# Loading b21 behind the third piece of a22, and b11's units in the order of their loading

## The chip, the core and the metric

The kernel runs on one core of one Trainium2 chip. The core has five engines with a queue of instructions each: TensorE (PE in the profile; matrix products), VectorE (DVE), ScalarE (ACT), GpSimd (POOL) and SyncE (SP). They run side by side and wait for each other by semaphores; within one engine the order of the program holds. Transfers between device memory and the on-chip memory are issued from the queues of SP, ACT and POOL, and 16 DMA engines carry them out. The metric is the time of one execution on the device in microseconds.

## The reference

```python
def reference(a, b, alpha):          # a, b: 4096 x 4096 float32, alpha = 0.01
    x = np.matmul(a, b)
    return np.where(x > 0, x, alpha * x)
```

A product of two square matrices, and a leaky ReLU on it.

## The kernel before

The output is cut into regions of 1024 x 1024. `g` (0 to 3) counts 1024 rows of A, called a group here, `j` (0 to 3) 1024 columns of B. The first region, (0, 0), is computed plainly. The other fifteen are taken in the order of the list `regions`: (0,1), (0,2), (0,3), then for each later group the columns 2, 0, 3, 1, and in the last group 2, 0, 1, 3. Counted from 0, regions 3, 7 and 11 are the first of their groups, 4, 8 and 12 the second, and 2, 6 and 10 are the "turning" ones, in which the next group of A comes in. The flags `turning`, `first_of_group` and `second_of_group` say so in the code.

A region is computed by Winograd's form of Strassen's method, with seven products instead of eight. A's part is cut into a11, a12, a21, a22 (512 rows by 2048 of k) and B's into b11, b12, b21, b22 (2048 of k by 512 columns). Sums of the quarters of A are s1 to s4, and sums of the quarters of B are made in place by DVE (`b_sum`, line 589), so that the tile of b11, for instance, holds b11 for product 0, then the sum t2 for product 2, then the sum for product 4. The products are listed in order:

```python
PRODUCTS = [("a11", 0, 0), ("a12", 1, 0), ("s2", 0, 0), ("s3", 0, 1), ("s1", 0, 0), ("a22", 1, 0), ("s4", 1, 1)]
```

Each entry names the operand of A and the quarter of B (half of k, half of the columns). Product 1 is a12 by b21, product 5 a22 by the sum that stands in b21's place. In regions that are not turning, and past group 0, some products are split once more into quarters of 256 (`fourth_in_quarters`, `sixth_in_quarters`, `seventh_in_quarters`, with the matmuls on line 752). Whole products have their matmuls on line 807: 64 of 128x128 by 128x512.

Every quarter of B has two units, k = 0 and 1, of 1024 rows of k: a tile of 128 x 8 x 512 in float16, 1 MB, in `b_pool`. A tag (`b11`, `b12`, `b21`, `b22`) has two buffers, so the two units of the next region's quarter take the buffers of the two units of this region's, and each load waits for the last product that reads its buffer. The variable `ks` is the order in which a region walks the units: (0, 1), or (1, 0) where the region before it was in quarters. So regions 4, 8 and 12 walk 1, 0; so do regions 6 and 10, while 7 and 11 walk 0, 1.

The order of the work is written by hand: every engine's queue has the order in which the code is written. `fetch_b(i + 1, quads, ks)` loads quarters of the next region's B through `fetch_unit`. For column 2 (`CACHED`), which is the first column of each later group, a unit comes from a float16 copy that an earlier region has left in device memory, as one transfer of 1 MB on SP's queue (line 528). For other columns it comes from B itself on POOL's queue, with the cast to float16 (line 533), or from another kept copy.

The next group of A comes in while a turning region is computed. It comes in four quarters of four pieces, 128 rows by 2048 of k each, in float16 0.5 MB. `fetch_a` issues a piece as four transfers on POOL's queue (line 133), into one of three buffers `a16`. `turn_a_in` transposes it on DVE (two instructions of line 142) and squares it on ACT (line 608; sums of squares that are tested later). `bring_a(1, 1, range(3))` does this for the first three pieces of a22, which is the last quarter to come in; the fourth follows after it.

What stands around the change is the end of a turning region. In the order of the code: product 4; the leaky ReLU and stores of one quarter of the output; `fetch_b` of b11; product 5 and its addition to the output quarter u2; `fetch_b` of b21; the three pieces of a22; `leave(u2_pairs, 1, 0)`, which runs the leaky ReLU on u2 (two DVE instructions, line 313) and issues four stores on SP (line 984); the sums of squares, the fourth piece and the sums s1 and s2 of the next group; product 6; `fetch_b` of b22; the copies of product 6's four PSUM banks on ACT (`keep`, line 820); and the last stores. The next region's product 1 writes the banks that these copies empty.

The order on SP at a turn is thus: b11 (two loads), b21 (two loads), the four stores of u2, b22 (two loads), four stores.

A small write by DVE has been used before to hold a load back: `load_s2(g, k, later=True)` sets one column of the tile on DVE (line 770), and the load that follows waits for it, and so for all that stands before it in DVE's queue. That load is on SP too.

Product 0 of regions past the first of a group is ordered by unit, then by pairs of row tiles:

```python
if n == 0 and late_s2:
    order = [(mt, k, c) for k in ks for mts in ((0, 1), (2, 3)) for c in range(KC) for mt in mts]
```

In regions 4, 8 and 12, b11 was loaded by the first region of the group, which walks its units 0, 1; product 0 walks them 1, 0. After product 0, DVE's sums go over the units in the order `ks` (lines 1049 to 1055): b12 minus b22 for a unit, then that added into b11 for the same unit.

Of the kernel before, what the change touches and what calls it, by code (L numbers as in the profile page):

```python
# [24 lines left out]
KC = 8  # L25
# [23 lines left out]
def kernel(  # L49
# [17 lines left out]
    nc = tc.nc  # L67
# [108 lines left out]
    def rows_of(mat, u, c, wide, whole):  # L176

        if u >= 2 or whole:
            per = 2 * KC
            k0 = u // 2 * 2 * KW  # L180
            c += u % 2 * KC
        else:
            per = KC // RUNS[u]
            k0 = u * KW + c // per * per * P
        return mat[k0:k0 + per * P, :].rearrange("(p c) n -> p c n", p=P)[:, c % per:c % per + wide, :]

    def b_rows(j, u, c, wide, nt=None, whole=False):

        n0 = j * 2 * NT + (nt or 0) * NT
        return rows_of(b[:, n0:n0 + (2 * NT if nt is None else NT)], u, c, wide, whole)  # L190
# [4 lines left out]
    def place(g, h, mt, j, nt):  # L195
        row = ((g * 2 + h) * MT + mt) * P
        col = (j * 2 + nt) * NT
        return out[row:row + P, col:col + NT]
# [4 lines left out]
    def a_cols(t, c, mt, is_plain=False):  # L203
        rows = slice(mt * P, (mt + 1) * P)
        return plain(t)[:, c, rows] if is_plain else t[:, c // 2, rows, c % 2]
# [106 lines left out]
    def leaky(t):  # L312
        nc.vector.scalar_tensor_tensor(t, t, alpha, t, op0=MULT, op1=MAX if alpha <= 1 else MIN)  # L313
# [24 lines left out]
    order = [("b", 0), ("a", 0, 0, 1), ("a", 1, 0, 1), ("a", 2, 0, 1), ("a", 3, 0, 1)]  # L338
# [3 lines left out]
    for what, i, *more in order:  # L342
        if what == "a":
            r, tiles = more
            k = slice(r * rw, (r + 1) * rw)
# [106 lines left out]
    for i in range(1, len(steps)):  # L452
        t, h, u, first, last = steps[i]
# [19 lines left out]
        t, h, u, first, last = steps[i]  # L473
# [34 lines left out]
    def fetch_b(i, quads, ks):  # L508

        if i >= len(regions):  # L510
            return
        for half, nt in quads:
            for k in ks:
                fetch_unit(i, 2 * half + k, nt)

    def move_t(name, t, k, out, queue=nc.sync):
        ends = kept_t[name][k], t.rearrange("p c n -> p (c n)")
        queue.dma_start(*(ends if out else ends[::-1]))

    def fetch_unit(i, u, nt):  # L520
        g, j = regions[i]
        half = u // 2
        t = b_pool.tile([P, KC, NT], DT, name="b", tag=f"b{half + 1}{nt + 1}")
        have_b[i, u, nt] = t
        if g > 1 and j == CACHED and (half, nt) == (0, 1):
            move_t("t3", t, u, False)
        elif g and j == CACHED:
            nc.sync.dma_start(t, rows_of(kept[nt], u, 0, KC, True))
        elif half and (g and j == LAST or g > 1 and j in OTHERS):
            nc.sync.dma_start(t.rearrange("p c n -> p (c n)"), kept_half[j][u - 2, nt])  # L530
        else:
            for c in range(0, KC, 4):
                nc.gpsimd.dma_start(t[:, c:c + 4, :], b_rows(j, u, c, 4, nt, g > 0))  # L533
            if j == CACHED:
                wide = KC // (RUNS + [1, 1])[u]
                for c in range(0, KC, wide):
                    nc.sync.dma_start(rows_of(kept[nt], u, c, wide, False), t[:, c:c + wide, :])
# [44 lines left out]
    def operand(g, name, k):  # L582
        if name[0] == "s":
            return s[g, name, k]
        return at[g, int(name[1]) - 1, 2 * (int(name[2]) - 1) + k]
# [5 lines left out]
    def measure(i, which, x, y):  # L591

        if which:
            tiles = [have_b[i, 2 * x + k, y] for k in ((1, 0) if regions[i][0] else (0, 1))]
        else:
            tiles = [at[regions[i][0], x, 2 * y + k] for k in range(2)]
        parts = halves(tiles[0]) + halves(tiles[1])
        if tiles[0] is first_a:
            return MeasureFirst(which, parts, None)
        return Measure(which, parts, not which)  # L600
# [181 lines left out]
    in_quarters = False  # L782
    for i, (g, j) in enumerate(regions):

        ks = (1, 0) if in_quarters else (0, 1)
        late_s2 = in_quarters
        final = i == len(regions) - 1
        turning = i + 1 < len(regions) and regions[i + 1][0] != g
# [8 lines left out]

        def product(n, banks, first):
            name, half, nt = PRODUCTS[n]
            todo = [(k, c) for k in ks for c in range(KC)]  # L800
            order = [(mt, k, c) for k, c in todo for mt in range(MT)]
            if n == 0 and late_s2:

                order = [(mt, k, c) for k in ks for mts in ((0, 1), (2, 3)) for c in range(KC) for mt in mts]
            for mt, k, c in order:
                t = operand(g, name, k)
                nc.tensor.matmul(  # L807
                    banks[mt], a_cols(t, c, mt, t is first_a), B(half, nt, k)[:, c, :],
                    start=first and (k, c) == todo[0], stop=(k, c) == todo[-1], skip_group_check=not first,
                )  # L810
# [160 lines left out]
        def add(acc, banks):  # L971
            for to, bank in zip(acc, banks):
                nc.vector.tensor_add(to, bank, to)  # L973
# [6 lines left out]
        def leave(pairs, h, nt):  # L980
            for r, t in enumerate(pairs):
                leaky(t.rearrange("p m n -> p (m n)"))
                for m in range(2):
                    nc.sync.dma_start(place(g, h, 2 * r + m, j, nt), t[:, m, :])

        if i == 0:
            for u, nt in ((2, 0), (2, 1), (3, 0), (3, 1)):
                fetch_unit(0, u, nt)
            for to, kept_part in stores:
                nc.gpsimd.dma_start(to, kept_part)  # L990
            sum_a(g, "s1")
            sum_a(g, "s2")
# [20 lines left out]
        def bring_a(h, half, some=range(MT)):  # L1013
            if turning:
                for n in some:
                    fetch_a(h, half, n)
                    turn_a_in(h, half, n)
# [7 lines left out]
        in_quarters = g > 0 and not turning  # L1025
        in_fourth = in_quarters and not first_of_group
        second_of_group = in_fourth and regions[i - 2][0] != g
# [3 lines left out]
        if first_of_group and g:  # L1031
            keep_s2(g)

        product(0, y, True)
        if second_of_group:
            sums_of_s3(g, (2,))
# [5 lines left out]
        if have_t2:  # L1042
            for k in ks:
                t = have_b[i, k, 0] = b_pool.tile([P, KC, NT], DT, name="b", tag="b11")
# [23 lines left out]
        bring_a(0, 0, range(3 if g else 4))  # L1068

        product(1, z, True)  # L1070
        add(u1, z)
        leave(u1_pairs, 0, 0)
# [25 lines left out]
        if not g:  # L1098
            bring_a(0, 1)

        product(2, y, False)
        if late_ones:
            late_ones[0].begin()
        u2_pairs, u2 = keep(y, 1 - side)
        if g:
            t = x_pool.tile([P, 4, QUARTER], DT, name="q", tag="x")
# [79 lines left out]
        if not in_quarters:  # L1186
            product(5, z, g > 0)
            add(u2[::-1], z[::-1])
        fetch_b(i + 1, [(1, 0)], (1, 0) if in_quarters else ks)
        bring_a(1, 1, range(3))  # L1190
        leave(u2_pairs, 1, 0)
        if sixth:
            sixth = measure(i + sixth[0], *sixth)
            sixth.begin()
            sixth.end()
# [33 lines left out]
    with tc.If(even == 0):  # L1229
        for m in range(M // RM):  # L1230
            a_blocks = []
            for u in range(KU):
                t = a_pool.tile([P, KC // 2, RM, 2], BF16, name="a", tag=f"a{u // 2 + 1}{m % 2 + 1}")
# [6 lines left out]
            for n in range(N // NT):  # L1240
                banks = [new_bank(n % 2 * 4 + mt) for mt in range(MT)]
                cols = slice(n * NT, (n + 1) * NT)
                for u in range(KU):
                    t = b_pool.tile([P, KC, NT], BF16, name="b", tag=f"b{u // 2 + 1}{n % 2 + 1}")
# [8 lines left out]
                for mt in range(MT):  # L1253
                    t = c_pool.tile([P, 2, NT], FP32, name="c", tag=f"c{side}")[:, 0]
# [44 lines left out]
```

## Time and profile before

| | us |
|---|---|
| median of 3 runs | 1534.99 (1533.63 to 1537.55) |
| the profiled execution's own time | 1536.2 |
| its span in the profile | 1534.2 |
| TensorE busy | 1524.3 |
| DVE busy | 1158.9 |
| ACT busy | 425.5 |
| POOL busy | 258.5 |

All times in the profile are counted from the start of the span. TensorE's granted clock is 0.999 of full speed. The matmuls are pipelined, and the end of one is modelled, so waits on TensorE are better read from the distance between starts. The regions that the change touches start on TensorE at these times: region 2 at 314.4, 3 at 411.1, 4 at 505.2, 6 at 689.5, 7 at 784.6, 8 at 878.1, 10 at 1062.1, 11 at 1157.6, 12 at 1251.7. The b loads that a line of the profile calls `b<-kept` are those from the kept copy; `a<-in_a_dram` are quarters of pieces of A. In the bytes by queue, `q1` is SP's queue, `q0` POOL's, `q10` ACT's.

### The profile page before, as it was taken

What the parts mean: (1) busy time and instruction counts of PE and PEld (TensorE: products, weight loads), DVE (VectorE), ACT (ScalarE), POOL (GpSimd) and SP (SyncE); (2) the same over time, 40 slices, a digit from 0 to 9 for tenths busy, and PEclk for the clock granted to TensorE, in tenths of its full rate; (3) what the DMA queues carried; (4) which work ended last, traced back from release to release, by engine and by line L of the source; (5) the groups of instructions that cost most, each with busy time, mean ns of one, the idle gap of its engine ahead of it and who ended that gap; (6) DMA issues with size and microseconds to landing.
All of it is one profiled execution on the core that took longest, in us unless ns stands there. A gap on an engine that the chain in (4) does not pass through costs nothing. (4 is left out here: it accounts for less than half of the span.)

```text
span 1534.2 us, 21785 instructions
## 1 busy us (share of the span) xinstructions
PE 1524.3 (99%) x8667; PEld 847.1 (55%) x8667; DVE 1158.9 (76%) x1207; ACT 425.5 (28%) x730; POOL 258.5 (17%) x426
## 2 busy tenths in 40 slices
PE   9999999999999999999999999999999999999998
PEld 4444444444446567574544747557544475746656
DVE  4368867765699686768769698676976987687677
ACT  2201344646310213103641130312464103041210
POOL 5641110143202011022220001010331100101000
PEclk9999999999999999999999999999999999999999
DMA  9999995998879999899797939669899892948723
GB/s 246 186 215 203 237 281 169 180 197 172 231 277 287 258 278 275 251 289 255 170 288 266 321 148 208 260 157 322 166 241 283 235 349 72 294 162 190 301 97 140
DMA packets 192002, 351.26 MB, mean 229 GB/s; under 512 B 18705, under 2 KB 131601, under 8 KB 178834
## 3 DMA queue, kind: packets, MB, share of 16 engines
q0 software_dynamic: 119808, 112.22, 46.2%
q1 hardware_dynamic: 65458, 211.98, 37.0%
q10 hardware_dynamic: 6624, 25.56, 4.4%
q8 instruction: 70, 1.15, 0.3%
q14 instruction: 42, 0.34, 0.1%
HBM read 344.98 MB, written 114.82 MB: 300 GB/s over the span
## 5 line engine op out<-in xcount | busy, mean ns | idle before, releaser
L807 PE MATMUL ps<-b,a 128*128 128x512 f16 x2624 | 571.1, 379 | 0.5 <-DMA b<-in_b_dram 0.3
L807 PE MATMUL ps<-b,s 128*128 128x512 f16 x2240 | 489.2, 379 | 0.0
L807 PEld LDWEIGHTS <-a 128*128 128x128 f16 x2624 | 256.7, 98 | 308.8 <-issue 1.5
L807 PEld LDWEIGHTS <-s 128*128 128x128 f16 x2240 | 219.1, 98 | 262.5 <-issue 0.4
L589 DVE TENSOR_TENSOR b<-b 128x4096 f16<-128x4096 f16 x104 | 234.6, 2286 | 42.7 <-DMA b<-in_b_dram 34.1
L533 POOL DMA_DIRECT2D b<-in_b_dram x128 | 94.9, 746 | 860.1 <-PE ps L752 437.2
L820 ACT COPY c<-ps 128x512 f32<-128x512 f32 x164 | 84.8, 596 | 469.1 <-PE ps L807 433.3
L142 DVE STREAM_TRANSPOSE a<-a 128x512 uint32<-128x512 uint32 (+2 forms) x120 | 127.0, 1106 | 100.8 <-DMA a<-in_a_dram 100.8
L133 POOL DMA_DIRECT2D a<-in_a_dram x252 | 137.6, 554 | 266.8 <-ACT junk L608 98.2
L608 ACT ACTIVATE junk<-a 128x512 bf16<-128x512 f16 x192 | 121.1, 631 | 99.1 <-DMA a<-in_a_dram 93.8
L752 PEld LDWEIGHTS <-q 128*128 128x128 f16 x1424 | 139.3, 98 | 16.7 <-issue 0.6
L313 DVE SCALAR_TENSOR_TENSOR c<-c 128x1024 f32<-128x1024 f32 (+2 forms) x123 | 141.5, 1190 | 3.8 <-ACT c L820 3.5
L973 DVE TENSOR_TENSOR c<-ps,c 128x512 f32<-128x512 f32 x140 | 87.5, 682 | 55.5 <-PE ps L807 41.8
L231 ACT ACTIVATE sq<-b 128x2048 bf16<-128x2048 f16 x64 | 118.3, 1910 | 37.1 <-DVE sq L240 29.4
L752 PEld LDWEIGHTS <-a 128*128 128x128 f16 x1200 | 117.4, 98 | 18.0 <-issue 0.4
L283 PE MATMUL ps<-b,a 128*128 128x512 f16 x512 | 112.4, 379 | 0.6 <-DVE part L324 0.2
L752 PE MATMUL ps<-b,q 128*128 128x256 f16 x784 | 92.0, 273 | 0.4 <-DVE c L862 0.4
L752 PE MATMUL ps<-b,a 128*128 128x256 f16 x752 | 88.3, 273 | 0.0
L283 PEld LDWEIGHTS <-a 128*128 128x128 f16 x512 | 49.7, 98 | 61.2 <-issue 2.1
L909 ACT COPY c<-ps 128x512 f32<-128x512 f32 x9 | 5.3, 586 | 269.7 <-PE ps L752 148.3
L752 PEld LDWEIGHTS <-s 128*128 128x128 f16 x624 | 61.0, 98 | 7.1
L862 DVE TENSOR_TENSOR c<-ps,c 128x512 f32<-128x512 f32 x80 | 52.2, 683 | 14.4 <-PE ps L752 14.4
(104 smaller groups left out, 904.8 us busy)
## 6 DMA issues: line engine op xcount, KB each, us to landing
b<-in_b_dram POOLq DMA_DIRECT2D x136, 512.0 KB, 11.7
out_dram<-c SPq DMA_DIRECT2D x240, 256.0 KB, 6.3
a<-in_a_dram POOLq DMA_DIRECT2D x244, 128.0 KB, 5.8
b<-kept_half SPq DMA_DIRECT2D x28, 1024.0 KB, 10.9
b<-kept SPq DMA_DIRECT2D x20, 1024.0 KB, 9.2
q<-kept_qs ACTq DMA_DIRECT2D x40, 512.0 KB, 7.8
s<-kept_s SPq DMA_DIRECT2D x18, 1024.0 KB, 7.7
q<-kept_qa SPq DMA_DIRECT2D x28, 512.0 KB, 7.3
```

The source lines that it names most:

```text
L133: nc.gpsimd.dma_start(a16[32 * q:32 * q + 32], src.rearrange("(g i) w -> i g w", i=32))
L142: nc.vector.transpose(part.rearrange("p c m e -> p c (m e)").bitcast(U32) .rearrange("p c (g i) -> p g c i", i=32), src[:, :, i * n:(i + 1 ...
L231: nc.scalar.activation(to, self.parts[n], SQUARE)
L283: nc.tensor.matmul(ps, a_cols(at[0, h, u], c, mt, (h, u) == (0, 0)), bt[0, u, nt][:, c, :], start=first, stop=last,)
L313: nc.vector.scalar_tensor_tensor(t, t, alpha, t, op0=MULT, op1=MAX if alpha <= 1 else MIN)
L533: nc.gpsimd.dma_start(t[:, c:c + 4, :], b_rows(j, u, c, 4, nt, g > 0))
L589: nc.vector.tensor_tensor(f(to), f(x0), f(x1), op)
L608: nc.scalar.activation(junk, piece[:, q, :], SQUARE, accum_out=to[:, 4 * n + q:4 * n + q + 1])
L752: nc.tensor.matmul(to[m], xq[:, c // 2, rows, c % 2], yq[:, c, :], start=first and c == 0 and m < banks, stop=c == KC - 1, skip_group_chec ...
L807: nc.tensor.matmul(banks[mt], a_cols(t, c, mt, t is first_a), B(half, nt, k)[:, c, :], start=first and (k, c) == todo[0], stop=(k, c) == t ...
L820: nc.scalar.copy(kept[mt], banks[mt])
L973: nc.vector.tensor_add(to, bank, to)
```

## The change

In turning regions the two loads of the next region's b21 are no longer issued right after product 5, but after the three pieces of a22 and the leaky ReLU and stores of u2. Each is preceded by a write of one column of its tile on DVE, so that SP issues the load only when DVE has come to that point. Other regions keep their order.

In product 0 of the second region of a group the units are walked 0, 1 instead of 1, 0. The DVE sums after it keep their order.

```diff
-    def fetch_unit(i, u, nt):
+    def fetch_unit(i, u, nt, later=False):
         g, j = regions[i]
         half = u // 2
         t = b_pool.tile([P, KC, NT], DT, name="b", tag=f"b{half + 1}{nt + 1}")
         have_b[i, u, nt] = t
+        if later:
+            nc.vector.memset(t[:, :1, :1], 0.0)
...
         def product(n, banks, first):
             name, half, nt = PRODUCTS[n]
-            todo = [(k, c) for k in ks for c in range(KC)]
+            ks_here = (0, 1) if n == 0 and second_of_group else ks
+            todo = [(k, c) for k in ks_here for c in range(KC)]
             order = [(mt, k, c) for k, c in todo for mt in range(MT)]
             if n == 0 and late_s2:
-                order = [(mt, k, c) for k in ks for mts in ((0, 1), (2, 3)) for c in range(KC) for mt in mts]
+                order = [(mt, k, c) for k in ks_here for mts in ((0, 1), (2, 3)) for c in range(KC) for mt in mts]
...
-        fetch_b(i + 1, [(1, 0)], (1, 0) if in_quarters else ks)
+        if not turning:
+            fetch_b(i + 1, [(1, 0)], (1, 0) if in_quarters else ks)
         bring_a(1, 1, range(3))
         leave(u2_pairs, 1, 0)
+        if turning:
+            for k in ks:
+                fetch_unit(i + 1, 2 + k, 0, True)
```

## The prediction

> **What bounds the kernel now.** I read the page's busy table first, then TensorE's timeline for gaps, then, around the three places where a group of A comes in, the timelines of DVE, SP and POOL, and the bytes by queue.
>
> ```profile
> span 1534.2 us, 21785 instructions
> PE 1524.3 (99%) x8667; PEld 847.1 (55%) x8667; DVE 1158.9 (76%) x1207; ACT 425.5 (28%) x730; POOL 258.5 (17%) x426
> ```
>
> The next lines are TensorE's timeline: start, length, line, tiles, count, and in brackets an idle time.
>
> ```profile
> 507.38 26.06 PE L807 MATMUL ps<-b,a 128*128 128x512 f16 x120 [0.31 <-DMA b<-in_b_dram]
> ...
> 784.62 27.79 PE L807 MATMUL ps<-b,a 128*128 128x512 f16 x128
> ...
> 1157.55 28.38 PE L807 MATMUL ps<-b,a 128*128 128x512 f16 x128
> ```
>
> TensorE is the bound, and it hardly ever waits. 128 matmuls of 512 columns take 27.79 us (0.216 us each) in region 7 and 28.38 us in region 11: 0.6 us of waiting, where product 1 of region 11 needs the PSUM banks that ScalarE copies out at 1170.5 to 1172.6. The bracket at 507.38 is region 4 waiting for the last piece of b11; by the starts of the matmuls on both sides the hole is 0.47 us. From 107 us to the end I find seven holes by start-to-start times, 2.1 us together. Nothing that only takes waits away can gain more than these 2.1 us, 0.14%.
>
> Now the third turn (regions 10 to 11), with the lines of SP, DVE and POOL in that order, each in a fence of its own:
>
> ```profile
> 1138.36 2.58 SPq L984 DMA_DIRECT2D out_dram<-c  x4
> 1141.17 3.08 SPq L528 DMA_DIRECT2D b<-kept  x4
> 1169.83 1.97 SPq L984 DMA_DIRECT2D out_dram<-c  x4
> 1171.89 1.00 SPq L528 DMA_DIRECT2D b<-kept  x2
> ```
>
> ```profile
> 1161.62 2.12 DVE L142 STREAM_TRANSPOSE a<-a 128x512 uint32<-128x512 uint32 x2 [13.54 <-DMA a<-in_a_dram]
> 1164.03 2.11 DVE L142 STREAM_TRANSPOSE a<-a 128x512 uint32<-128x512 uint32 x2 [0.29 <-DMA a<-in_a_dram]
> 1166.59 2.11 DVE L142 STREAM_TRANSPOSE a<-a 128x512 uint32<-128x512 uint32 x2 [0.45 <-DMA a<-in_a_dram]
> 1168.61 2.33 DVE L313 SCALAR_TENSOR_TENSOR c<-c 128x1024 f32<-128x1024 f32 x2
> ```
>
> ```profile
> 1142.04 4.29 POOL L133 DMA_DIRECT2D a<-in_a_dram  x8 [3.91 <-ACT junk L608]
> 1151.93 0.54 POOL L133 DMA_DIRECT2D a<-in_a_dram  x1 [5.61 <-DMA a<-in_a_dram]
> 1154.92 0.55 POOL L133 DMA_DIRECT2D a<-in_a_dram  x1 [2.45 <-DMA a<-in_a_dram]
> 1158.81 0.54 POOL L133 DMA_DIRECT2D a<-in_a_dram  x1 [3.35 <-DMA a<-in_a_dram]
> 1161.78 0.55 POOL L133 DMA_DIRECT2D a<-in_a_dram  x1 [2.43 <-DMA a<-in_a_dram]
> ```
>
> The x4 of SP at 1141.17 are b11 (two units) and b21 (two units); the x2 at 1171.89 are b22. DVE sits idle 13.5 us until the first piece of a22 is there. POOL has issued eight quarter pieces and the next four go out one at a time, each when an earlier one has landed: eight are in flight at most. The bytes by queue say why the pieces are slow; first the stretch 1146 to 1152, with b on SP's queue (q1) beside a on POOL's (q0), then 1158 to 1161, a alone:
>
> ```profile
> q1 hardware_dynamic: 262, 1.88, 78.3%
> q0 software_dynamic: 249, 0.24, 25.1%
> ...
> q0 software_dynamic: 623, 0.57, 115.9%
> ```
>
> Beside b, A gets 0.04 MB/us; alone 0.19. A piece is 0.5 MB.
>
> **The change, part by part.** Working against the profiled execution: its own time is 1536.2 us, 2.0 above its span and 1.2 above the median of 1534.99.
>
> *b21 moved behind the a22 pieces (three turns).* Removed from their place: six SP issues of 1 MB. Added: six memsets on DVE, 59 ns each by the nine rows of line 770, 0.12 us a turn. They run right after the leaky of u2; DVE has 13.5 us of idle time shortly before, so they cost TensorE nothing, and without that cover 0.35 us. POOL's and ScalarE's queues keep their orders. On SP the four u2 stores no longer stand behind b21 (no gain, they wait for the leaky); b22's two loads and the next stores now stand behind b21.
>
> First, how much earlier is a22? Up to the landing of b11's second unit nothing changes, since b21 is behind b11 on the same queue. By the landing records that unit is in at 777.4 (second turn) and 1150.6 (third) on the median DMA engine; on the last, 778.2 and 1152.2. Of twelve quarter pieces one is in by then and the second a quarter or less. The rest come at 0.128 MB / 0.19 = 0.65 us each (the landings in that stretch are 0.6 to 0.65 apart): some 10.8 x 0.65 = 7.0 us, so the median engine ends at 784.4 and 1157.6. The slowest engine lags 1.1 in the second turn and 1.7 in the third at that point. POOL's pacing is no limit: the twelfth issue needs the fourth quarter landed, 780.3 and 1154.1, and 2.6 us to the first bytes. So the third piece is in at 785.5 and 1159.3; before it was 790.6 and 1166.5. In the first turn, in the same way, 408.3 instead of 413.5.
>
> Then b21. From the landing of the third piece to the first u2 store of SP there are 3.36 us in all three turns (1166.47 to 1169.83: two transposes of 1.05 and the first leaky of 1.16). From the first store, 1 MB of stores and two loads of 1 MB must pass. The nearest row is b22 in the first turn, which goes this way now with nothing beside it: the stores begin at 416.91, the loads land at 425.07 and 427.54, which is 8.2 and 10.6 us later. In the other turns it is 12.3, because the t2 loads of ScalarE's queue run beside it; those wait for the end of product 0, so they come after b21. I take 10.6 and keep 12.3 as the far end; the near end is 9.5, 2.5 us for each of three MB at the observed spacing plus 2 us.
>
> - First turn: b21's first unit is in at 408.3 + 3.4 + 8.2 = 419.9, wanted at product 1, 411.05 + 13.81 = 424.9; the second unit at 422.3, wanted at 431.8. No cost.
> - Second turn: here the units come in the order 1, 0 (region 6 walks them so), while product 1 of region 7 starts with 0. It is in at 785.5 + 3.4 + 10.6 = 799.5, wanted at 784.62 + 13.81 = 798.4: a stall of 1.1 us.
> - Third turn: likewise 1159.3 + 3.4 + 10.6 = 1173.3, wanted at 1171.4: 1.9 us.
>
> In SP's queue behind b21, b22 is held up next. In region 3 DVE wants it at 431.25; it lands near 427, as now. In regions 7 and 11 its first reader is the DVE sum at 822 and 1198, over 10 us away.
>
> The Trainium skill, page "DMA: Bandwidth & Descriptors", section "Anatomy of one DMA — SWDGE (gpsimd) path", gives about 2.0 us fixed and then bytes at 436 GB/s. By it the 3.1 MB would take an estimated 9.2 us instead of 10.6, the stalls would be 0 and 0.5 us, and the sum below would come to a gain of 0.6 us; the trace's 10.6 decides here.
>
> What goes: the 0.6 us wait at 1171.4. ScalarE's bank copies are behind the squares of the three a22 pieces (3.0 us a piece). With pieces at 1154.1, 1156.7 and 1159.3 the copies run at about 1163 to 1165, far ahead of 1171.4. What is late next is b21 itself.
>
> *Product 0 of regions 4, 8 and 12 takes unit 0 first.* No instruction is added. b11's unit 0 is loaded before unit 1, so the wait at 507 goes: 0.47 us; regions 8 and 12 show no wait there. Against it, DVE's sum into b11's unit 1 now waits for the end of product 0 instead of its middle. In region 4 that sum runs at 530.6 and in region 8 at 903.4, after product 0 has ended (519 and 892): nothing. In region 12 it runs at 1261.3 and must wait until 1265.5, 4.2 us, and three sums (6.9 us) end at 1272.4 instead of 1268.1. Behind them the measure and the add of u1 slip by some 1.4 us and are caught up in DVE's idle 2.84 us at 1290.5. Product 2 wants the sums at 1279.3: 6.9 us of cover. If it were gone, 4.2 us at most.
>
> *Sum.* -0.6 - 0.5 + 1.1 + 1.9 = +1.9 us: 1538.1 on the profiled execution's own time, 1536.8 against the median. With the near end of the unknown (9.5) the stalls are 0 and 0.8 and the sum is -0.3; with the far end (12.3) they are 2.8 and 3.6 and it is +5.3.
>
> **The rivals.**
>
> *No new wait.* If the slowest DMA engine does not lag (it may be this execution's own), the third pieces are in at 784.4 and 1157.6 and b21 at 798.4 and 1171.6: 0.2 us of stall, a gain of 0.9, 1534.1. For it: the first turn's landings recover within 1 us once queues are empty. Against: the lag is in all three turns.
>
> *Slower: a22 comes little earlier, and b21 is what TensorE waits for.* Place: product 1 of regions 7 and 11. If POOL's pacing and not b's bytes held the pieces, they would land as now, and b21 at 804.5 and 1180.4: stalls of 6.1 and 9.1, 0.2 in the first turn, in all +14.3, 1549.3. Against it stand 0.04 beside 0.19 MB/us; for it, the four single issues 3 to 4 us apart. The forecast has little room: each microsecond that the third piece is later than I say costs 2 us over the two turns, and 1.4 us decide, for the sum then passes 4.6 us.
> A long stall may cost again: the first eleven matmuls of the kernel take 4.87 us, 0.44 each, twice the later pace. The Trainium skill, page "TensorE: Matmul & The Clock Gate", Part 1, has the clock halved after about 3.4 us of idleness and back after as much work; no hole here is long enough to show it, and by that rule I would estimate 1.7 us more for each of the two stalls.
>
> *The reordered product 0 bites.* DVE's slip in region 12 reaches TensorE at product 2: +4.2 - 1.1, with b21 as forecast 1541. The 6.9 us of cover speak against it.
>
> *Faster by more than the holes.* It would need a faster clock, and the granted clock is already 0.999 of full speed.
>
> **How the numbers follow.** About 0.3%, 4.6 us, is what a measurement of this kernel can tell from no change (its three runs span 3.9 us). Forecast 0.53 (up to +4.6); no new wait 0.17; slower through b21 0.24; through the reordering 0.03; faster over 0.3% 0.03. So within 0.3%: 0.70; slower 0.27; faster 0.03. The range takes the gain of 1.1 and a little noise at the low end, 1533.6, and reaches to +8.5, well into the slower case, 1543.5.
>
> **What would show each step.** Right: b21's two loads on SP directly after the u2 stores; a22's first transpose near 1154 instead of 1161.6 and the third near 1159.4; no hole at 507; holes of 1 to 2 us ended by a b load near 798.4 and 1171.4, none in region 3. Wrong: the third transposes still later than 787 and 1161, or b21 landing over 12 us after the first store, or holes at product 2 of region 12.

## The result, and the profile after

The changed kernel takes 1546.8 us (median of 6 runs, 1544.71 to 1550.07), the kernel before 1535.12 us on the same occasion. The ratio is 1.0077, with a 95% interval of 1.0061 to 1.0093: slower by 11.7 us. The forecast of 1536.8 us and its range up to 1543.5 us both missed. The profiled execution took 1544.71 us, with a span of 1542.8 us. It is the fastest of the six: its span is 8.6 us above that of the kernel before, 3 us less than the medians differ.

TensorE's timeline of the changed kernel, with products 0, 1 and 2 of region 7 and then of region 11, where the view cuts product 2 off (line 807 of before is line 812 here):

```profile
783.11 13.98 PE L812 MATMUL ps<-b,a 128*128 128x512 f16 x64
801.91 15.47 PE L812 MATMUL ps<-b,a 128*128 128x512 f16 x64 [4.82 <-DVE c L313]
817.22 13.98 PE L812 MATMUL ps<-b,s 128*128 128x512 f16 x64
...
1162.19 13.98 PE L812 MATMUL ps<-b,a 128*128 128x512 f16 x64
1179.99 15.66 PE L812 MATMUL ps<-b,a 128*128 128x512 f16 x64 [3.83 <-DMA b<-kept]
1195.49 9.88 PE L812 MATMUL ps<-b,s 128*128 128x512 f16 x45
```

A product of 64 matmuls takes 13.81 us from its first start to the next product's. Product 1 was due at 783.11 + 13.81 = 796.92 and started at 801.91, 4.99 us late; in region 11 it was due at 1176.00 and started at 1179.99, 3.99 us late. In both places product 1 itself took longer, 15.31 and 15.50 us, which is 1.50 and 1.69 us more. Together 12.2 us, all in two places. Less the 2.1 us of holes of the kernel before, nearly all of them gone, and 1.5 us by which this execution is shorter before 109 us and after the last matmul, that is the 8.6 us of the spans. In region 3 there is no hole; the hole at 507 is gone. The bracket of the first hole names a leaky ReLU of DVE. But the unit of b21 that is loaded second, unit 0, which product 1 reads first, landed at 801.77, 0.13 us ahead of the start, and in the third turn at 1179.86, again 0.13 ahead; the runs below show that it is the load that counts.

SP's queue in the second turn and in the third:

```profile
788.47 1.97 SPq L989 DMA_DIRECT2D out_dram<-c  x4
790.55 2.30 SPq L531 DMA_DIRECT2D b<-kept  x4
...
1167.90 1.97 SPq L989 DMA_DIRECT2D out_dram<-c  x4
1169.98 2.05 SPq L531 DMA_DIRECT2D b<-kept  x4
```

The x4 are now b21 and b22 in one go, behind the stores of u2, as the change says. Next DVE in the second turn: the transposes of the second and third pieces, the leaky of u2, and the two writes that hold b21 back (a sum of statistics between them is left out).

```profile
782.71 2.10 DVE L142 STREAM_TRANSPOSE a<-a 128x512 uint32<-128x512 uint32 x2 [0.50 <-DMA a<-in_a_dram]
785.24 2.10 DVE L142 STREAM_TRANSPOSE a<-a 128x512 uint32<-128x512 uint32 x2 [0.42 <-DMA a<-in_a_dram]
787.25 2.33 DVE L313 SCALAR_TENSOR_TENSOR c<-c 128x1024 f32<-128x1024 f32 x2
...
789.53 0.07 DVE L527 MEMSET b<- 128x1 f16 x2
```

So a22 does come earlier. Counted from the start of the next region, the third piece's transposes start 2.1 us into it (785.24 against 783.11), where it was 6.1 us before (790.69 against 784.62); in the third turn 2.5 us (1164.66 against 1162.19) instead of 9.0.

Two more views name what the forecast had not counted. ScalarE's queue, with the first load of t2:

```profile
793.21 0.63 ACT L611 ACTIVATE junk<-a 128x512 bf16<-128x512 f16 x1
793.35 0.33 ACTq L518 DMA_DIRECT2D b<-kept_t  x1
793.74 0.19 ACT L611 ACTIVATION_READ_ACCUMULATOR junk<-a 128x1 f32 x1
797.12 0.33 ACTq L518 DMA_DIRECT2D b<-kept_t  x1
```

The first t2 load is issued in the middle of product 0, between the issue of b21 (790.55 on) and its landing. And the table by stretches of time over product 1 of region 7, whose columns are the stretch, its length, busy time and count for each engine, the granted clock, the DMA share and GB/s:

```profile
801.90:805.30 3.40, 3.39 (x9) 1.24 (x10) 3.40 (x6) 0.00 (x0) 0.00 (x0) 0.55 1.02 429
805.30:808.70 3.40, 3.40 (x17) 1.57 (x16) 3.40 (x3) 0.00 (x0) 0.00 (x0) 1.00 0.98 357
```

Right behind the hole nine matmuls fit where seventeen fit later, at a granted clock of 0.55. By the clock's records it is 0.5 for 3.41 us from 801.56, and again for 3.41 us from 1180.44.

### The profile page after: what moved, and what is told of

Its sections match the earlier page's. It is cut to its first block, busy times and chain, and to the rows that moved or that the text cites. A ratio compares the mean times of both kernels' runs of the same rounds, so it can differ in the third digit from the quotient of the medians.

```text
span 1542.8 us, 21794 instructions
## 1 busy us (share of the span) xinstructions
PE 1526.9 (99%) x8667; PEld 847.8 (55%) x8667; DVE 1159.5 (75%) x1213; ACT 425.6 (28%) x730; POOL 258.2 (17%) x426
## 4 chain that ended last, share of the span: by engine, by line
PE 90%; DMA 5%; DVE 2%; ACT 1%; issue 1%; POOL 0%; SPq 0%; DVEq 0%; ACTq 0%
PE ps L812 61%; PE ps L755 22%; PE ps L283 7%; DMA a<-in_a_dram 4%; ACT junk L611 1%; DVE a L142 1%; DMA b<-kept 1%; DVE s L562 1%; POOL a L133 0%; DMA a_in<-in_a_dram 0%; DVE b L592 0%; DVE c L313 0%; PE turned L373 0%; DVE c L943 0%; DVE q L690 0%
## 6 DMA issues: line engine op xcount, KB each, us to landing
b<-in_b_dram POOLq DMA_DIRECT2D x136, 512.0 KB, 10.8
```

## The experiments

Theory 1: all of the loss is TensorE waiting at product 1 of regions 7 and 11 for the unit of b21 that it reads first and that is loaded second. The rivals: the reordered product 0 (theory 2), the crowd of transfers in the new place whichever unit comes first (theory 3), SP's queue being slow without t2 (theory 4). Theories 5 and 6 are about the slow product 1 after the wait. Every ratio is to the kernel before, run on the same chip.

### The two halves of the change

The reordered product 0 alone; `fetch_b` of b21 is where it was:

```diff
-        if not turning:
-            fetch_b(i + 1, [(1, 0)], (1, 0) if in_quarters else ks)
+        fetch_b(i + 1, [(1, 0)], (1, 0) if in_quarters else ks)
...
-        if turning:
-            for k in ks:
-                fetch_unit(i + 1, 2 + k, 0, True)
```

> Only the reordered product 0 of regions 4, 8 and 12; b21 is loaded right after product 5 as before. Theory 1 (TensorE waits for b21's second unit at product 1 of regions 7 and 11, and the whole loss is there): the 0.47 us hole near 507 is gone, the 0.6 us wait near 1171 stays, no new hole: 1534.6 us, 0.5 below the kernel before, which three rounds cannot tell from it. Theory 2 (DVE's slip in region 12 from the reordering is a good part of the loss): 4 us or more above the kernel before, with a hole at product 2 of region 12.

Measured: 1533.91 us, ratio 0.9996 (0.9984 to 1.0008). DVE in region 12, of this kernel:

```profile
1259.23 0.06 DVE L773 MEMSET s<- 128x1 f16 x1
1263.79 6.82 DVE L592 TENSOR_TENSOR b<-b 128x4096 f16<-128x4096 f16 x3 [4.50 <-PE ps L812]
```

DVE waits 4.5 us for the end of product 0, and TensorE has no hole in region 12: the slip is caught up. The hole at 507 is gone. The wait near 1171, which was expected to stay, is not there in this execution, though b21 is loaded in its old place. Whether it comes and goes from one execution to the next or went with the reordering is open: one execution of each kernel was profiled. Theory 2 falls.

b21 alone; product 0 keeps its order:

```diff
-            ks_here = (0, 1) if n == 0 and second_of_group else ks
+            ks_here = ks
```

> Only b21 moved; product 0 keeps the order 1, 0. Theory 1: as the changed kernel or 0.5 us slower, about 1547 us (ratio to before 1.007 to 1.009), two holes of 4 to 5 us at product 1 of regions 7 and 11, each followed by matmuls at half clock for 3.4 us. Theory 2: within 3 us of the kernel before.

Measured: 1546.75 us, ratio 1.0066 (1.0043 to 1.0088). Product 1 starts 4.3 us late in region 7 (801.28, due at 796.96) and 4.8 us in region 11 (1181.25, due at 1176.50). At region 11 half clock lasted 6.83 us, twice what was expected. The hole near 507 did not come back with the old order: the piece of b11 that product 0 of region 4 waited for landed at 500.01, before that product began at 504.18, while in the kernel before it landed at 507.33. In the run with the reordering alone it landed at 505.59, and the old order would have wanted it at 504.68 + 8 x 0.216 = 506.41. So no run shows the reordering itself taking a hole away. The loss is the move of b21.

### The units in the order of their reader

```diff
-            for k in ks:
+            for k in (0, 1):
                 fetch_unit(i + 1, 2 + k, 0, True)
```

> The changed kernel, but the two units of b21 are loaded in the order 0, 1, which is the order of product 1 that reads them. Theory 1: TensorE waits only for the unit it reads first. The first of the two loads landed at 797.4 and 1176.3 where product 1 was due at 796.9 and 1176.0, so holes of 0.5 and 0.3 us are left, too short for the clock to fall, and the second unit has another 6.9 us: 1535 us, ratio 0.999 to 1.001. Theory 3 (not the order but the crowd of transfers in the new place delays product 1, whichever unit comes first): holes stay at 3 us or more each, 1543 us or more.

Measured: 1534.68 us, ratio 0.9993 (0.9983 to 1.0002). TensorE's products 0 and 1 of regions 7 and 11, in this kernel:

```profile
784.00 27.79 PE L812 MATMUL ps<-b,a 128*128 128x512 f16 x128
...
1157.83 27.79 PE L812 MATMUL ps<-b,a 128*128 128x512 f16 x128
```

No hole at all. The transfers are the same and as crowded: in region 7 the second load of b21 landed at 801.81 here, 10.7 us after its issue, as in the changed kernel. The first one, now unit 0, landed at 796.63, where product 1 was due at 784.00 + 13.81 = 797.81; in region 11 it landed at 1170.65, due at 1171.64. One swapped pair takes the whole loss away, and theory 3 falls.

### Ahead of the leaky and the stores

```diff
         bring_a(1, 1, range(3))
-        leave(u2_pairs, 1, 0)
         if turning:
             for k in ks:
                 fetch_unit(i + 1, 2 + k, 0, True)
+        leave(u2_pairs, 1, 0)
```

> The changed kernel, but b21 is loaded right behind the transposes of the third a22 piece and ahead of the leaky and the stores of u2, still in the order 1, 0. Theory 1: the loads are issued 3.1 us earlier (two leaky instructions and most of the store issues) and 1 MB less stands ahead of them, some 5 us in all: the second unit lands at about 795.5 to 797.2 and 1175 by the changed kernel's clock, against 796.9 and 1176.0: holes of 0 to 0.5 us, 1534.5 to 1536 us. Theory 3: with the stores behind instead of ahead the same bytes are in flight, holes of 2 us or more stay, 1539 us or more.

Measured: 1535.45 us, ratio 0.9998 (0.9988 to 1.0007). In the profiled execution, the slowest of ten at 1537.3 us, product 1 starts 0.63 and 1.52 us late:

```profile
800.12 13.97 PE L812 MATMUL ps<-b,a 128*128 128x512 f16 x64 [0.46 <-DMA b<-kept]
...
1174.24 13.97 PE L812 MATMUL ps<-b,a 128*128 128x512 f16 x64 [1.36 <-DMA b<-kept]
```

In the third turn the hole is 1 us longer than theory 1 allowed, since the landing was 1174.11, 10.3 us after its issue, where some 8 were reckoned. The direction holds: 1 MB of stores and two leaky instructions less ahead of b21 bring nearly all of the loss back even in the wrong order. And after these short holes product 1 takes its normal time.

### t2 held back

```diff
                 t = have_b[i, k, 0] = b_pool.tile([P, KC, NT], DT, name="b", tag="b11")
+                nc.vector.memset(t[:, :1, :1], 0.0)
                 move_t("t2", t, k, False, nc.scalar)
```

> The changed kernel, with the two loads of t2 on ScalarE's queue (regions 7 and 11) held back by a write of one column on DVE, which DVE reaches some 8 us later, after the leaky ReLU of the last stores of the region before. Theory 1 with its size explained by t2 (in the changed kernel a t2 load is issued at 793.35, in the middle of product 0, and shares the DMA engines with b21's second unit): the second unit lands 10.6 to 11 us after the first u2 store instead of 13.3 and 12.0, so the holes at product 1 shrink from 5.0 and 4.0 to some 2.4 and 2.7 us; no hole then spans long enough for the clock to halve, which takes another 3.2 us away: about 1539 us, ratio 1.002 to 1.004. Rival theory 4 (b21 is slow in SP's queue by itself, t2 does not matter): holes and time stay, 1545 to 1548 us.

Measured: 1541.39 us, ratio 1.0045 (1.0027 to 1.0062).

```profile
800.49 13.97 PE L812 MATMUL ps<-b,a 128*128 128x512 f16 x64 [2.58 <-DMA b<-kept]
...
1176.89 15.66 PE L812 MATMUL ps<-b,a 128*128 128x512 f16 x64 [3.65 <-DMA b<-kept]
```

With t2 issued at 803.5, the second unit landed 11.4 us after the first u2 store in the second turn (788.96 to 800.35) and 10.8 us in the third (1165.95 to 1176.76), against 13.3 and 12.0 in the changed kernel. The same interval in the three other kernels with b21 in its new place behind the stores and t2 free is 13.1 to 13.3 us in the second turn and 11.8 to 12.6 in the third, so the difference is not that of one execution. In the first turn, which has no t2 load, it is 10.0 to 11.4 us in these five kernels. The bytes by queue agree: from 796.5 us to the landing, ScalarE's queue moved 1.01 MB and SP's 1.29 MB in 5.3 us in the changed kernel, and with t2 held SP's alone moved 1.62 MB in 3.9 us. So t2's share is 1.2 to 1.9 us of the wait, and theory 4 falls. The second turn went as expected, with a hole of 2.74 us and no fall of the clock. The third did not: the first store came 6.7 us into region 11, 1.0 us later than in the changed kernel, the hole stayed at 3.8 us, and the clock fell behind it (0.5 for 3.41 us from 1177.43). That cost 1.7 us of product 1 in the profiled execution, most of the 2 us by which the median is above what was expected; the five executions range from 1537.0 to 1545.1 us.

### TensorE kept busy through the wait

```diff
+        for n in range(20 if have_t2 else 0):
+            nc.tensor.matmul(z[n % MT], a_cols(operand(g, "a12", 0), n % KC, n % MT), B(0, 1, 0)[:, n % KC, :],
+                             start=True, stop=True)
         product(1, z, True)
```

> The changed kernel, with 20 extra matmuls (128x128 by 128x512, 4.3 us) on TensorE ahead of product 1 in regions 7 and 11, on tiles that are long there, into the banks that product 1 then overwrites. They fill most of the wait for b21 and change nothing else. Theory 5 (product 1 runs 1.5 to 1.7 us slower after the wait because TensorE was idle and its clock halved): product 1 takes its normal 13.8 us again from start to start, no stretch at half clock inside the kernel, 3 us less than the changed kernel: about 1543.5 us, ratio 1.005 to 1.007. Rival theory 6 (product 1 is slow because of the transfers that land beside it): product 1 still takes 15.3 us or more from start to start, and the time stays at 1546 to 1548 us, or rises where the wait is shorter than 4.3 us.

Measured: 1542.68 us, ratio 1.0049 (1.0028 to 1.0069), some 4 us below the changed kernel by the medians, though the two intervals overlap a little (1.0061 to 1.0093 there). TensorE in region 7 of this kernel, then the same stretch of the table by time as above:

```profile
797.34 4.48 PE L1076 MATMUL ps<-b,a 128*128 128x512 f16 x20
801.65 13.98 PE L812 MATMUL ps<-b,a 128*128 128x512 f16 x64
...
801.90:805.30 3.40, 3.40 (x17) 1.54 (x16) 3.40 (x3) 0.00 (x0) 0.00 (x0) 1.00 1.01 419
```

Product 1 starts as soon as the extra matmuls end, 4.3 us late in both regions, and runs at its normal pace: seventeen matmuls in the stretch where the changed kernel had nine, with the DMA engines as busy (419 and 429 GB/s), and the granted clock stays at 1. Theory 6 falls: the slow product was the clock after an idle TensorE, not the transfers. In this execution b21's unit 0 landed earlier than in the changed kernel, at 800.35 and 1178.21, 1.3 and 1.5 us before the extra matmuls ended. Without them the waits would have been an estimated 3.1 and 3.0 us (from the landings and the 0.13 us to the start), so here the extra matmuls took longer than the waits that they covered, and whether the clock would have fallen in this execution is not known.

### Both mendings

```diff
         bring_a(1, 1, range(3))
-        leave(u2_pairs, 1, 0)
         if turning:
-            for k in ks:
+            for k in (0, 1):
                 fetch_unit(i + 1, 2 + k, 0, True)
+        leave(u2_pairs, 1, 0)
```

> Both mendings together: b21 ahead of the leaky and the stores of u2, and its units in the order 0, 1. Theory 1: both units land ahead of their reader by 3 us or more, no hole at product 1 in any run, and of the holes of the kernel before the one at 507 is gone: 1533.5 to 1535 us, 0.3 to 1 us below the kernel before, ratio 0.9990 to 1.0003. Theory 3 (crowding as such): 1538 us or more.

Measured: 1533.61 us (11 runs, 1532.68 to 1534.49), ratio 0.9992 (0.9983 to 1.0001). No hole at product 1, no fall of the clock, and 0.9 us of holes in all past 107 us, where the kernel before had 2.1. It is at least as good as the kernel before; that it is better is not settled, for the interval reaches just past 1.

## Why the prediction was wrong

The place and the mechanism were named, and the first turn costs nothing, as forecast; the two stalls were sized at 1.1 and 1.9 us and came to 5.0 and 4.0, with another 1.5 and 1.7 us of slow matmuls that the sum did not have at all. Step by step, second turn and third, the first two rows counted from the start of the next region:

| step | forecast | measured |
|---|---|---|
| third piece of a22 landed | 0.9 and 1.7 | 2.0 and 2.3 |
| first u2 store | 4.2 and 5.1 | 5.4 and 5.7 |
| from that store to unit 0 of b21 | 10.6 and 10.6 | 13.3 and 12.0 |
| product 1 late by | 1.1 and 1.9 | 5.0 and 4.0 |
| product 1 longer by | nothing | 1.5 and 1.7 |

The first load of t2 in region 7 of the kernel before, on ScalarE's queue:

```profile
799.36 0.33 ACTq L518 DMA_DIRECT2D b<-kept_t  x1
```

- **The step that failed: 10.6 us, because the t2 loads "wait for the end of product 0, so they come after b21".** They don't. The first of them was issued at 793.35, in the middle of product 0, when ScalarE had come to it (in the third turn at 1173.19, where product 0 ended at 1176.2); only the second waited for the end. In the kernel before, ScalarE came to these loads behind squares of the last a22 piece, when product 0 had ended at 798.4, so nothing in that trace contradicted me. But a22 coming earlier makes ScalarE earlier too, and so t2 collides with the very load that the change had moved there. Holding t2 back gives 11.4 and 10.8, near the 10.6, and a time of 1541.4 us, inside the range. The far end of 12.3 that I kept was the better row. The traces show that the buffer of the first t2 load is free at half of product 0: TensorE raised the semaphore that both loads wait for at 790.19, at the half, and at 797.10, at the end; the first load went out between the two, the second 0.02 us after the end. Why it is given that buffer I have not settled.
- **The landing of a22** was sized well: 4.0 and 6.6 us earlier, counted from the next region's start, where I had 5.1 and 7.2. POOL's pacing, the rival's mechanism, was no limit: its single issues became a run of three once b21 was away, and the quarter pieces landed 0.4 to 0.7 us apart to the end. But 1.1 and 0.6 us of error go into the stalls in full. I had said that 1.4 us decide, and still gave the slower case 0.24.
- **The clock** stood beside the slow rival only, with 1.7 us for each stall; the sum had nothing for it. With the errors above, the holes grew past the length at which it falls, and 3.2 us came on top.
- **What goes:** the hole at 507 went, but in the run that moves b21 alone as well: in all seven kernels with b21 moved b11's piece landed between 500.0 and 502.6 instead of 507.33. Why it lands earlier there is open, and what the reordering is worth was not shown. The 0.6 us near 1171 also went, but it is not in the profiled execution with the reordering alone and b21 in its old place either. The reordering costs nothing, as forecast: DVE's wait was 4.5 us, forecast 4.2, and was caught up.
- **The bound on gains**, 2.1 us of holes, held: the best version of all is 0.6 us below the kernel before by the medians.
- The extra from these rows: 2.7 + 1.4 from the store to the landing (of it 1.9 + 1.2 are t2's, by the run that holds it back), 1.1 + 0.6 from a22, 1.5 + 1.7 from the clock: 9.0 us on top of the 3.0 of stalls that I had. That is 12.0 us; the 0.13 us from each landing to the start of product 1, which the sum left out, brings it to the 12.2 us that the trace shows, within rounding.

The Trainium skill's rule of 2.0 us plus bytes at 436 GB/s ("DMA: Bandwidth & Descriptors", section "Anatomy of one DMA — SWDGE (gpsimd) path"), weighed in the prediction, is given there for a single transfer issued from GpSimd, and these are six on SP's queue. It would have made the wait shorter still: an estimated 9.2 us for what took 10.8 to 11.4 without t2 beside it. Here the measurement decides.

## What to carry to other kernels

When a load is moved close to its reader, put first what the reader reads first: here the order of two 1 MB loads was worth the whole 12 us. A load that waits on an engine's position inherits everything before that position, so hold it back behind the instruction that matters and not behind the stores that follow. And before counting a queue's transfers as later, ask what else the change makes earlier: an engine that is freed sooner issues its own loads sooner.

## What the runs showed that I had not expected

A wait of TensorE of 3.8 us or more cost twice here. The holes of 0.6, 1.5 and 2.74 us at product 1 were followed by matmuls at the normal pace; those of 3.8, 4.0, 4.3 and 5.0 us by 3.41 us at a granted clock of 0.5, and the 4.8 us hole in region 11 of the run with b21 alone by 6.83 us. No profiled hole at product 1 was between 2.74 and 3.8 us long. These bounds agree with the Trainium skill, page "TensorE: Matmul & The Clock Gate", Part 1, which has the clock halved after about 3.4 us of idleness and back after as much work; the 6.83 us are longer than that. By the clock's records its changes lie whole multiples of 3.413 us apart (from 801.56 to 1180.44 in the changed kernel 111 of them), not at a fixed distance from the hole. With twenty useless matmuls in the wait, product 1 kept its pace; the kernel with them is some 4 us below the changed one by the medians, with the reservations made above.

A copy with a cast from POOL's queue got little beside plain loads from SP's: 0.04 MB/us against 0.31 in the same stretch of the kernel before, and 0.19 MB/us alone. Taking 2 MB of the plain loads out of its way brought 1.5 MB of A in 4.0 and 6.6 us sooner in the second and third turns, about what those 2 MB take on their own: 5 us at the 2.5 us between the landings of two queued loads in the first turn.
